# A two-layer diffusion block on one core: loads ahead of the first block in one row, filter network first, small loads and spectrum reloads on GpSimd's queue

## The chip, the core and the metric

The kernel runs on one core of a Trainium2 chip. The metric is device time in microseconds of one launch, the median of several runs. Before the change it is 1902.57 us (three runs, 1902.44 to 1904.87). One execution was also recorded by the hardware profiler; all rows of profiles are from such executions, and their times count from the first instruction of the span.

A core has five engines that run side by side, each with its own queue of instructions that it works off in order: TensorE (matmuls; PE in the profile, its weight loads PEld), VectorE (DVE), ScalarE (ACT), GpSimd (POOL) and SyncE (SP, which here only issues DMAs). ScalarE and GpSimd can issue DMAs too, each from its own queue. Engines wait for each other and for DMAs by semaphores.

## The reference, cut to what matters

Two token streams, `x` (256 tokens, "latent") and `ctx` (256 tokens), width 1024, go through two layers. Each layer is a half feed-forward block, a mixer and a second half feed-forward block. All in float32.

```python
s_l, s_c = silu(c), silu(c_ctx)
for layer in range(2):
    need_ctx = layer < 1
    mod_l = (s_l @ mod_w[layer] + mod_b[layer]).reshape(1, 9, 1, 1024)     # and mod_c from s_c
    lat = lat + 0.5 * mod_l[:, 2] * swiglu(adaln_in(lat, g[0], mod_l, 0), w1, w3, w2)   # same for ctx
    h_l = adaln_in(lat, g[1], mod_l, 1)                                    # same for ctx
    y_l, y_c = mixer_ab(h_l, h_c, ...) if layer == 0 else mixer_c(h_l, h_c, ...)
    lat = macaron(lat + mod_l[:, 5] * y_l, g[2], mod_l, 2, ...)            # ctx in layer 0 only
return rmsnorm(lat, final_norm_w)

def adaln_in(h, gain, mod, k):
    return rmsnorm(h, gain) * (1.0 + mod[:, 3 * k + 1]) + mod[:, 3 * k]

def hyena_filters(n, f_w0, f_b0, f_w1, f_b1, f_freq, f_wout):
    hid = sin(f_freq * (z @ f_w0 + f_b0))
    for i in range(2):
        hid = sin(f_freq * (hid @ f_w1[i] + f_b1[i]))
    return (hid @ f_wout).reshape(n, 2, 2, 512) * window

def long_conv_bidir(v, h_fwd, h_bwd, skip):          # used twice in mixer_ab, per stream
    taps_f = rfft(concat([h_fwd, 0, reversed h_bwd]), n=2 * n)
    return irfft(rfft(v, n=2 * n) * taps_f)[:n] + v * skip
```

The filters of the long convolution depend on weights alone, not on tokens, and so does the modulation (on `c`, `c_ctx` and the weights). Both can be computed before the first feed-forward block.

## The kernel before, in words

Activations stand transposed: width over the 128 partitions, in 8 chunks of 128, tokens along the row (512: latent, then context). The residual is the eight tiles `res`. For precision each float32 matmul of the big products is made of three in a faster format: every operand is split into a high and a low part (`split`, L149: ScalarE copies the high part at L151, VectorE subtracts at L152), and `mm3` (L154 to L157) multiplies high by high, high by low and low by high. That is why L155, L156 and L157 carry most of TensorE's time. Small or early products stay float32.

**The opening** is what comes ahead of `ffn(0, 0, ...)`, written at L1070 to L1092:

- constants and the filter network's inputs (`cst` L161, `w0` L171 to L173) are loaded by SyncE; rows of biases and of `c`, `c_ctx` into `crow` (L177, L179) by ScalarE; norm weights and biases into `prow` and `mrow` (L200, L214) mostly by GpSimd. Small transposes on TensorE (L182, L205, L216) turn them into columns; `fcol` (L184) holds the network's biases, `sF` (L187) the silu of `c`, `c_ctx`.
- `load_x(s)` (L329) loads 1 MB of one stream and transposes it into `res` (L335, L336). `Adaln.stats` (L464) computes the norm's scale: squares (L437), sums (L439), two matmuls, a power on GpSimd (L447).
- `mod_group` (L242) computes one eighth of the modulation rows 1 and 0: two loads of 512 KB (`mw`, L256) and per load two float32 matmuls that use 32 columns of TensorE each (L259), the profile counts four; the four column groups of the two loads differ. After eight groups the sums are gathered (`part` L264, L268) and `modT` is written (L233).
- `filter_hidden` (L359) is the filter network: three layers of matmul (L365, L367), range reduction on VectorE (L369 to L375) and sine on ScalarE (L378, L382). `filter_tables` (L345) loads the output weights `wo`, the window `win`, the skips and the transform tables. `filter_taps` (L389) makes the taps (L395 to L402), `filter_spectra` (L404) their spectra by matmuls, 60 in all, scales them (L418, L419, L425) and stores them to DRAM from ScalarE's queue (`TR`, `TI`, `TN`, L426 to L428).
- `ffn_first` (L521) loads and splits the first weights of the feed-forward block; `Adaln.stream(s)` (L467) writes its normalized input `h` (L482 to L484), which needs `modT`.

**After it** come the feed-forward blocks, 11 slices of 256 hidden columns each, with weights streamed by SyncE; the rest of the modulation is spread over them (`mod_row`, L271). In `mixer_ab` the spectra come back from DRAM: `tn` at L903 and L904, `tf` in `load_filters` at L787 and L788, both by SyncE, into the pool `fp` of three buffers; the products with the token spectra use them at L819 and L820.

**What sets the order.** The program names no order across engines and no addresses. A planner runs the whole program once on its own cost model with the numbers of buffers that the pools name (`bufs=`); then each engine's queue is ordered: of what is ready in the plan, first what the plan can least afford to delay. Loads are queued as soon as the plan has room for their tile, so `tn` is loaded back some 500 us before its use. Tiles get addresses from their planned lifetimes; two tiles whose planned lifetimes don't overlap may share memory, and then the later one's writer waits for the earlier one's readers.

Of the kernel before, what the change touches and what calls it, by code (L numbers as in the profile page):

```python
# [97 lines left out]
def tile_dit(ctx: ExitStack, tc: tile.TileContext, a: dict, out: bass.AP, dbg=None):  # L98
# [4 lines left out]
    big = ctx.enter_context(tc.tile_pool(name="big", bufs=1))  # L103
    wp = ctx.enter_context(tc.tile_pool(name="wp", bufs=4))
    hp = ctx.enter_context(tc.tile_pool(name="hp", bufs=8))
    gp = ctx.enter_context(tc.tile_pool(name="gp", bufs=10))
    mp = ctx.enter_context(tc.tile_pool(name="mp", bufs=6))
    fp = ctx.enter_context(tc.tile_pool(name="fp", bufs=3))
    tp = ctx.enter_context(tc.tile_pool(name="tp", bufs=NT))
    xp = ctx.enter_context(tc.tile_pool(name="xp", bufs=6))  # L110
    sp = ctx.enter_context(tc.tile_pool(name="sp", bufs=2))
# [81 lines left out]
    for nm, src, n in (  # L193
# [6 lines left out]
        (nc.scalar if nm == "nw" else nc.gpsimd).dma_start(prow[r : r + n, : src.shape[1]], src)  # L200
# [960 lines left out]
```

## Time and profile before

| what | value |
|---|---|
| median of three runs | 1902.57 us (1902.44 to 1904.87) |
| the profiled execution's own time | 1902.08 us |
| its span, first to last instruction | 1900.3 us |
| instructions | 25792 |
| busy share of TensorE, VectorE, ScalarE, GpSimd | 97%, 66%, 39%, 4% |
| bytes moved | 271.65 MB, mean 143 GB/s |
| granted clock of TensorE | 0.990 |

"Busy" is the share of the span in which an engine has an instruction in work; issuing DMAs does not count. Matmuls are pipelined and their ends are modelled, so that neighbours overlap in the rows. In rows of groups "x64 | 15.0, 604 | 2.9 <-DMA" reads: 64 instructions, together busy 15.0 us, mean of one 604 ns, and 2.9 us in which the engine stood idle just before them, ended by a DMA. In rows of waits "14.5, 7, 3.9" are total, number of times and longest wait in us. A DMA row ends with the size of each transfer and the median us from issue to landing.

### The profile page before, as it was taken

What the parts mean: (1) busy time and instruction counts of PE and PEld (TensorE: products, weight loads), DVE (VectorE), ACT (ScalarE), POOL (GpSimd) and SP (SyncE); (2) the same over time, 40 slices, a digit from 0 to 9 for tenths busy, and PEclk for the clock granted to TensorE, in tenths of its full rate; (3) what the DMA queues carried; (4) which work ended last, traced back from release to release, by engine and by line L of the source; (5) the groups of instructions that cost most, each with busy time, mean ns of one, the idle gap of its engine ahead of it and who ended that gap; (6) DMA issues with size and microseconds to landing.
All of it is one profiled execution on the core that took longest, in us unless ns stands there. A gap on an engine that the chain in (4) does not pass through costs nothing.

```text
span 1900.3 us, 25792 instructions
## 1 busy us (share of the span) xinstructions
PE 1850.6 (97%) x10358; PEld 1566.0 (82%) x10358; DVE 1257.0 (66%) x1972; ACT 738.0 (39%) x1190; POOL 73.6 (4%) x63
## 2 busy tenths in 40 slices
PE   7999999999999998999999999999999999989998
PEld 3868788889878788888888897887888988889998
DVE  5557686776666795877767358655344866667665
ACT  4533233224555433432332234222322566654443
POOL 1000000000100002000000110000000100020000
PEclk9999999999999999999999999999999999989998
DMA  8675555351323332545554325443323233335551
GB/s 267 216 245 177 171 186 208 127 191 45 122 88 100 104 109 84 195 170 175 197 184 143 111 78 176 173 160 113 111 89 119 54 106 84 106 111 178 200 188 57
DMA packets 191009, 271.65 MB, mean 143 GB/s; under 512 B 19688, under 2 KB 139755, under 8 KB 190889
## 3 DMA queue, kind: packets, MB, share of 16 engines
q1 hardware_dynamic: 189324, 267.63, 42.7%
q10 hardware_dynamic: 1260, 2.14, 0.3%
q8 instruction: 81, 1.33, 0.3%
q14 instruction: 40, 0.32, 0.1%
q0 software_dynamic: 304, 0.24, 0.0%
HBM read 262.63 MB, written 7.34 MB: 142 GB/s over the span
## 4 chain that ended last, share of the span: by engine, by line
PE 67%; DVE 4%; ACT 2%; issue 1%; POOL 1%; DMA 0%; SPq 0%; DVEq 0%; ACTq 0%
PE pu L155 11%; PE pu L156 11%; PE pu L157 11%; PE pd L155 7%; PE pd L157 7%; PE pd L156 7%; PE ps L155 3%; PE ps L156 3%; PE ps L157 3%; PE pu L1012 1%; DVE wl L152 1%; PE ps L667 1%; DVE acc L439 1%; PE pu L982 1%; PE ps L293 1%
## 5 line engine op out<-in xcount | busy, mean ns | idle before, releaser
L157 PE MATMUL pu<-h,wl 128*128 128x512 f32 (+1 forms) x1600 | 545.6, 342 | 3.0 <-POOL wl L152 3.0
L155 PE MATMUL pu<-h,wh 128*128 128x512 f32 (+1 forms) x1600 | 545.0, 342 | 1.6 <-ACT h L483 1.5
L156 PE MATMUL pu<-h,wh 128*128 128x512 f32 (+1 forms) x1600 | 546.0, 342 | 0.1
L151 ACT ACTIVATE wh<-raw 128x1024 fp32r<-128x1024 f32 x228 | 240.3, 1058 | 558.6 <-PE pu L156 403.2
L152 DVE TENSOR_TENSOR wl<-raw,wh 128x1024 fp32r<-128x1024 f32 x216 | 263.7, 1225 | 203.8 <-ACT wh L151 177.6
L155 PEld LDWEIGHTS pu<-h,wh 128*128 128x128 f32 x1600 | 303.8, 191 | 44.1 <-issue 4.2
L157 PEld LDWEIGHTS pu<-h,wl 128*128 128x128 f32 x1600 | 304.7, 191 | 38.4 <-POOL wl L152 3.3
L156 PEld LDWEIGHTS pu<-h,wh 128*128 128x128 f32 x1600 | 304.9, 191 | 33.8 <-DVE h L484 0.5
L282 DVE SCALAR_TENSOR_TENSOR mv<-mw,sF,mv 128x1024 f32<-128x1024 f32 x210 | 258.5, 1279 | 20.5 <-DMA mw<-in_mod_w_dram 16.2
L151 ACT ACTIVATE w<-raw 128x1024 fp32r<-128x1024 f32 x88 | 91.5, 1057 | 164.2 <-PE ps L156 120.5
L510 DVE SCALAR_TENSOR_TENSOR res<-pd,gate,res 128x256 f32<-128x256 f32 x244 | 110.7, 479 | 40.5 <-PE pd L157 40.0
L547 DVE TENSOR_TENSOR sg<-sg,pu 128x512 f32<-128x512 f32 (+1 forms) x87 | 52.2, 603 | 127.4 <-PE pu L157 125.0
L152 DVE TENSOR_TENSOR w<-raw,w 128x1024 fp32r<-128x1024 f32 x88 | 107.0, 1221 | 42.0 <-ACT w L151 41.9
L155 PE MATMUL pd<-g,w 128*128 128x512 f32 (+1 forms) x376 | 133.6, 355 | 0.0
L157 PE MATMUL pd<-g,w 128*128 128x512 f32 (+1 forms) x376 | 132.6, 353 | 0.0
L156 PE MATMUL pd<-g,w 128*128 128x512 f32 (+1 forms) x376 | 132.6, 353 | 0.0
L155 PE MATMUL ps<-g,w 128*128 128x512 f32 (+1 forms) x320 | 116.3, 363 | 0.0
L157 PE MATMUL ps<-g,w 128*128 128x512 f32 (+1 forms) x320 | 116.1, 363 | 0.0
L156 PE MATMUL ps<-g,w 128*128 128x512 f32 (+1 forms) x320 | 116.1, 363 | 0.0
L155 PE MATMUL pd<-h,wh 128*128 128x512 f32 (+1 forms) x288 | 108.3, 376 | 1.9 <-ACT e L989 0.9
L157 PE MATMUL pd<-h,wl 128*128 128x512 f32 (+1 forms) x288 | 107.6, 374 | 1.7 <-DVE wl L152 1.7
L156 PE MATMUL pd<-h,wh 128*128 128x512 f32 (+1 forms) x288 | 106.9, 371 | 0.0
(256 smaller groups left out, 2726.0 us busy)
## 6 DMA issues: line engine op xcount, KB each, us to landing
raw<-in_ffn_w_dram SPq DMA_DIRECT2D x132, 1024.0 KB, 5.3
mw<-in_mod_w_dram SPq DMA_DIRECT2D x144, 512.0 KB, 6.0
raw<-in_ab_w_in_dram SPq DMA_DIRECT2D x12, 1024.0 KB, 6.9
raw<-in_na_w_in_dram SPq DMA_DIRECT2D x12, 1024.0 KB, 5.0
raw<-in_ab_w_out_dram SPq DMA_DIRECT2D x4, 1024.0 KB
raw<-in_na_w_out_dram SPq DMA_DIRECT2D x4, 1024.0 KB, 5.5
bias<-in_na_rpb_dram SPq DMA_DIRECT2D x32, 96.0 KB, 6.1
dftr<-const_dft_dram SPq DMA_DIRECT2D x5, 256.0 KB
```

The lines of the kernel that those rows point to most:

```text
L151: S.activation(hi, src, AF.Copy)
L152: eng.tensor_tensor(lo, src, hi.bitcast(F32), op=ALU.subtract)
L155: nc.tensor.matmul(ps, wh, xh, start=start, stop=False)
L156: nc.tensor.matmul(ps, wh, xl, start=False, stop=False)
L157: nc.tensor.matmul(ps, wl, xh, start=False, stop=stop)
L282: V.scalar_tensor_tensor(acc, mw, c, acc, op0=ALU.mult, op1=ALU.add)
L293: nc.tensor.matmul(ps[32 * j : 32 * j + 32], row[:, 31 - b : 63 - b], mod_acc[l, i][j % 2][:, j // 2], start=b == 0, stop=b == len(batch) ...
L439: V.tensor_tensor(acc, acc, q, op=ALU.add)
L510: V.scalar_tensor_tensor(res[d][:, sl], ps[:, po], g[:, d, s : s + 1], res[d][:, sl], op0=ALU.mult, op1=ALU.add)
L547: V.tensor_tensor(sg[:, sl], sg[:, sl], p3[:, sl], op=ALU.mult)
L667: nc.tensor.transpose(at[kt // 2][:, o : o + P], e[:, P * kt : P * kt + P], ident)
L982: nc.tensor.matmul(pss[m], x[pr, qsl], y[pr], start=n == 0, stop=n == 2)
```

## The change

In words:

- The 16 loads of the modulation weights for rows 1 and 0 get two tiles of their own (pool `mwp`, 32 KB per partition each) and are written out ahead: eight for row 1 after `x`, the other eight after `ctx`. `mod_group` then finds its weights there. The loads of `x` and `ctx` are parted from their transposes (`load_x`, `take_x`).
- The filter network comes first, ahead of the transposes of `x`; the output weights and the window are loaded at the start from ScalarE's queue, the former in two loads in place of four. The modulation groups are spread by two, two, one, one, two between taps and spectra.
- `crow` and all of `prow` are loaded from GpSimd's queue; the two rows of `f_b1` in one load.
- `tn` and `tf` are loaded back by GpSimd in place of SyncE.
- The small constant tiles and `res` become slices of one tile `kept`. All other SBUF pools go through a wrapper that asks for addresses aligned to the size (up to 2048 bytes).

```diff
+class _Pool:
+    def tile(self, shape, dt, **kw):
+        size = 4 * math.prod(shape[1:])
+        if size >= 1024:
+            kw["align_bytes"] = min(size & -size, 2048)
+        return self.pool.tile(shape, dt, **kw)
...
+    mwp = _Pool(ctx.enter_context(tc.tile_pool(name="mwp", bufs=2)))
...
+    kept = const.tile([P, KEPT_W], F32, name="kept")
+    def keep(w):
+        used[0] += w
+        return kept[:, used[0] - w : used[0]]
...
-        nc.scalar.dma_start(crow[8 * s : 8 * s + 8, :P], src)
-    for r, src in ((16, a["hy_f_b0"]), (17, a["hy_f_b1"][0, 0:1]), (18, a["hy_f_b1"][0, 1:2]), (19, a["hy_f_freq"])):
-        nc.scalar.dma_start(crow[r : r + 1, :64], src)
+        nc.gpsimd.dma_start(crow[8 * s : 8 * s + 8, :P], src)
+    for r, src in ((16, a["hy_f_b0"]), (17, a["hy_f_b1"][0]), (19, a["hy_f_freq"])):
+        nc.gpsimd.dma_start(crow[r : r + src.shape[0], :64], src)
...
-        (nc.scalar if nm == "nw" else nc.gpsimd).dma_start(prow[r : r + n, : src.shape[1]], src)
+        nc.gpsimd.dma_start(prow[r : r + n, : src.shape[1]], src)
...
-    res = [big.tile([P, TOK], F32, name=f"res{d}") for d in range(NDC)]
+    res = [keep(TOK) for d in range(NDC)]
...
+    mod_rest = {}
+    def mod_load(l, i, g, mws=None):
+        mws = mws or [gp.tile([P, 2, 512], F32, tag="g", name="mw") for _ in range(2)]
+        for c in range(2):
+            k0 = 4 * (g % 2) + 2 * c
+            nc.sync.dma_start(mws[c], mod_rows(l, i, k0, 2, (512 * (g // 2), 512 * (g // 2) + 512)).rearrange("(k p) f -> p k f", p=P))
+        return mws
+    mwa = [mwp.tile([P, 8, 2, 512], F32, tag="mw", name="mw") for _ in range(2)]
+    def mod_ahead(n, l, i):
+        for g in range(4):
+            mod_rest[i, g] = mod_load(l, i, g, [mwa[g // 2][:, 4 * n + 2 * (g % 2) + c] for c in range(2)])
...
-        for c in range(2):
+        mws = mod_rest.pop((i, g), None) or mod_load(l, i, g)
+        for c, mw in enumerate(mws):
             k0 = 4 * (g % 2) + 2 * c
-            mw = gp.tile([P, 2, 512], F32, tag="g", name="mw")
-            nc.sync.dma_start(mw, mod_rows(l, i, k0, 2, (512 * (g // 2), 512 * (g // 2) + 512)).rearrange("(k p) f -> p k f", p=P))
...
-        wo = M(F32, name="wo")
-        for o in range(2):
-            for i in range(2):
-                nc.sync.dma_start(wo[o][64 * i : 64 * i + 64], a["hy_f_wout"][0][:, 1024 * o + 512 * i : 1024 * o + 512 * i + 512])
+        wo = mp.tile([P, 2, TOK], F32, tag="m", name="wo")
+        src = a["hy_f_wout"][0].rearrange("j (o i c) -> j o i c", o=2, i=2)
+        for i in range(2):
+            nc.scalar.dma_start(wo[64 * i : 64 * i + 64], src[:, :, i])
         win = fp.tile([P, 2, TOK], F32, tag="f", name="win")
-        nc.sync.dma_start(win, a["win"].rearrange("p (a c) -> p a c", a=2))
+        nc.scalar.dma_start(win, a["win"].rearrange("p (a c) -> p a c", a=2))
...
-                nc.sync.dma_start(tf[o, f][0], TR[o][f])
-                nc.sync.dma_start(tf[o, f][1], TI[o][f])
+                nc.gpsimd.dma_start(tf[o, f][0], TR[o][f])
+                nc.gpsimd.dma_start(tf[o, f][1], TI[o][f])
...
-            nc.sync.dma_start(tn[o][1:], TR[o][0][1:])
-            nc.sync.dma_start(tn[o][0:1], TN[o])
+            nc.gpsimd.dma_start(tn[o][1:], TR[o][0][1:])
+            nc.gpsimd.dma_start(tn[o][0:1], TN[o])
...
-    load_x(0)
-    mod_some(1)
-    load_x(1)
-    ads[0, 0].stats(0)
-    mod_some(1)
-    ads[0, 0].stats(1)
-    hid = filter_hidden(w0)
-    mod_some(1)
-    mod_some(1)
-    mod_some(1)
-    flt = filter_tables()
-    filter_taps(0, PU, hid, *flt)
-    mod_some(1)
-    filter_taps(1, PU, hid, *flt)
-    mod_some(1)
-    mod_some(1)
-    filter_spectra(0, (0,), PU, flt[-1])
-    first = ffn_first(0, 0)
-    ads[0, 0].stream(0)
-    filter_spectra(0, (1,), PU, flt[-1])
-    filter_spectra(1, (0,), PU, flt[-1])
-    filter_spectra(1, (1,), PU, flt[-1])
-    ads[0, 0].stream(1)
+    xin = load_x(0)
+    flt = filter_tables()
+    mod_ahead(0, 0, 1)
+    cin = load_x(1)
+    mod_ahead(1, 0, 0)
+    hid = filter_hidden(w0)
+    take_x(0, xin)
+    mod_some(2)
+    take_x(1, cin)
+    ads[0, 0].stats(0)
+    ads[0, 0].stats(1)
+    filter_taps(0, PU, hid, *flt)
+    mod_some(2)
+    filter_taps(1, PU, hid, *flt)
+    filter_spectra(0, (0,), PU, flt[-1])
+    mod_some(1)
+    filter_spectra(0, (1,), PU, flt[-1])
+    mod_some(1)
+    first = ffn_first(0, 0)
+    filter_spectra(1, (0,), PU, flt[-1])
+    mod_some(2)
+    ads[0, 0].stream(0)
+    filter_spectra(1, (1,), PU, flt[-1])
+    ads[0, 0].stream(1)
```

More of the change, by code (lines that the diff above doesn't have):

```diff
@@ L44 @@
 CST_W = _n
+KEPT_W = CST_W + NDC * TOK + 920
 def constants():
@@ L102, in tile_dit @@
     const = ctx.enter_context(tc.tile_pool(name="const", bufs=1))
[L103 to L111, printed above, removed]
+    wp = _Pool(ctx.enter_context(tc.tile_pool(name="wp", bufs=4)))
+    hp = _Pool(ctx.enter_context(tc.tile_pool(name="hp", bufs=8)))
+    gp = _Pool(ctx.enter_context(tc.tile_pool(name="gp", bufs=10)))
+    mp = _Pool(ctx.enter_context(tc.tile_pool(name="mp", bufs=6)))
+    fp = _Pool(ctx.enter_context(tc.tile_pool(name="fp", bufs=3)))
+    tp = _Pool(ctx.enter_context(tc.tile_pool(name="tp", bufs=NT)))
+    mwp = _Pool(ctx.enter_context(tc.tile_pool(name="mwp", bufs=2)))
+    xp = _Pool(ctx.enter_context(tc.tile_pool(name="xp", bufs=6)))
+    sp = _Pool(ctx.enter_context(tc.tile_pool(name="sp", bufs=2)))
     pu = ctx.enter_context(tc.tile_pool(name="pu", bufs=4, space=PSUM))
@@ L157, in mm3 @@
         nc.tensor.matmul(ps, wl, xh, start=False, stop=stop)
-    cst = const.tile([P, CST_W], F32, name="cst")
+    kept = const.tile([P, KEPT_W], F32, name="kept")
+    used = [0]
+    def keep(w):
+        used[0] += w
+        return kept[:, used[0] - w : used[0]]
+    cst = keep(CST_W)
     nc.sync.dma_start(cst, a["cst"])
@@ L165, in tile_dit @@
     wf = cst[:, _CO["wf"]]
-    ones = const.tile([P, 1], F32, name="ones")
+    ones = keep(1)
     V.memset(ones, 1.0)
-    nhalf = const.tile([P, 32], F32, name="nhalf")
+    nhalf = keep(32)
     V.memset(nhalf, -0.5)
@@ L176, in tile_dit @@
     for s, src in enumerate((a["c"].rearrange("o (k p) -> (o k) p", p=P), a["c_ctx"].rearrange("(k p) -> k p", p=P))):
-        nc.scalar.dma_start(crow[8 * s : 8 * s + 8, :P], src)
-    for r, src in ((16, a["hy_f_b0"]), (17, a["hy_f_b1"][0, 0:1]), (18, a["hy_f_b1"][0, 1:2]), (19, a["hy_f_freq"])):
-        nc.scalar.dma_start(crow[r : r + 1, :64], src)
+        nc.gpsimd.dma_start(crow[8 * s : 8 * s + 8, :P], src)
+    for r, src in ((16, a["hy_f_b0"]), (17, a["hy_f_b1"][0]), (19, a["hy_f_freq"])):
+        nc.gpsimd.dma_start(crow[r : r + src.shape[0], :64], src)
     pst = PS()
     nc.tensor.transpose(pst[:, :20], crow[:20, :P], ident[:20, :20])
-    fcol = const.tile([P, 4], F32, name="fcol")
+    fcol = keep(4)
     V.tensor_copy(fcol, pst[:, 16:20])
-    sF = const.tile([P, NDC, 38], F32, name="sF")
+    sF = keep(NDC * 38).rearrange("p (k f) -> p k f", k=NDC)
     V.memset(sF, 0.0)
@@ L217, in tile_dit @@
         V.tensor_copy(modb[:, l], pst[:, :72])
-    res = [big.tile([P, TOK], F32, name=f"res{d}") for d in range(NDC)]
-    modT = [const.tile([P, 72, 2], F32, name=f"modT{l}") for l in range(2)]
+    res = [keep(TOK) for d in range(NDC)]
+    modT = [keep(144).rearrange("p (k s) -> p k s", s=2) for l in range(2)]
     def raw():
@@ L331, in load_x, with take_x @@
         nc.sync.dma_start(xin, a[("x", "ctx")[s]][0].rearrange("(t p) c -> p t c", p=P))
+        return xin
+    def take_x(s, xin):
         for d in range(NDC):
@@ L356, in filter_tables @@
         tables(2, lambda i: tab[i][0], lambda i: tab[i][1])
-        return wo, [win[:, 0], win[:, 1]], skip, tab
+        return [wo[:, 0], wo[:, 1]], [win[:, 0], win[:, 1]], skip, tab
     def filter_hidden(w0):
@@ L519, in span, with ffn_first @@
         return slice(LAT * streams[0], LAT * streams[-1] + LAT)
-    def ffn_first(l, j, eng=V):
-        r1, r3 = [wload(a[nm][l, j][:, :FB]) for nm in ("ffn_w1", "ffn_w3")]
+    def ffn_first(l, j, eng=V, rs=None):
+        r1, r3 = rs or [wload(a[nm][l, j][:, :FB]) for nm in ("ffn_w1", "ffn_w3")]
         return [whalf(r[:, :, P * c : P * c + P], "w", eng=eng) for c in range(2) for r in (r1, r3)]
```

14 lines of the change are left out of this document (7 added, 7 removed).

## The prediction

> **What bounds the kernel now.** I read the page first (busy time, slices, chain), then the first 130 us by stages, then the groups of TensorE and the queue waits of the opening, and last the places where moved loads are used. Times are microseconds of the profiled execution.
>
> ```profile
> span 1900.3 us, 25792 instructions
> PE 1850.6 (97%) x10358; PEld 1566.0 (82%) x10358; DVE 1257.0 (66%) x1972; ACT 738.0 (39%) x1190; POOL 73.6 (4%) x63
> PE   7999999999999998999999999999999999989998
> PE 67%; DVE 4%; ACT 2%; issue 1%; POOL 1%; DMA 0%; SPq 0%; DVEq 0%; ACTq 0%
> ```
>
> TensorE is busy 97% of the span and carries the chain that ended last; DMA has 0% of that chain. Only the first slice is below 8. So a change in the loads can pay in the opening and hardly anywhere else. The same table of busy time, cut by hand at the first matmul, the first filter tap and the first matmul of the first feed-forward block (columns: stretch, length, then busy us and count of PE, PEld, DVE, ACT, POOL; granted clock, DMA share, GB/s):
>
> ```profile
> 0.00:7.68 7.68, 0.00 (x0) 0.00 (x0) 0.71 (x5) 0.47 (x1) 3.53 (x10) 1.00 0.58 175
> 7.68:33.38 25.70, 20.38 (x107) 10.56 (x107) 13.49 (x42) 14.30 (x42) 2.40 (x4) 1.00 0.87 297
> 33.38:63.58 30.20, 30.20 (x108) 15.98 (x109) 20.22 (x36) 15.83 (x26) 0.00 (x0) 0.94 0.76 243
> 63.58:1900.30 1836.72, 1800.06 (x10146) 1539.46 (x10144) 1222.59 (x1890) 707.34 (x1123) 67.71 (x49) 0.99 0.42 139
> ```
>
> The first block starts at 63.58. Before it TensorE waits 7.68 for its first operand, then is idle 25.70 − 20.38 = 5.32, and from the first tap on it is never idle: 30.20 of 30.20. The opening is therefore bound by TensorE from 33.38 on, and before that by what it waits for. The granted clock is 0.94 in the last stage; at full clock the same work would take about 30.20 × 0.06 = 1.8 less. What the work is, in the groups of TensorE up to 63.58 and, last row, of the stage from 33.38 on:
>
> ```profile
> L259 PE MATMUL ps<-mw,sF 128*32 128x512 f32 x64 | 15.0, 604 | 2.9 <-DMA mw<-in_mod_w_dram 2.9
> L395 PE MATMUL pu<-wo,hid 128*128 128x512 f32 x16 | 9.3, 727 | 0.2 <-PE ps L259 0.2
> L335 PE MATMUL pu<-cst,raw 128*128 128x128 f32 x32 | 6.1, 348 | 0.8 <-ACT sq L437 0.8
> L365 PE MATMUL pd<-w 33*64 33x256 f32 x2 | 1.1, 657 | 7.7 <-DMA w<-const_tmp_dram 7.7
> L268 PE MATMUL ps<-cst,part 128*128 128x8 f32 x8 | 1.0, 255 | 0.0
> L259 PE MATMUL ps<-mw,sF 128*32 128x512 f32 x24 | 6.3, 604 | 0.0
> ```
>
> Modulation (L259) costs 15.0 and the taps (L395) 9.3, clock loss included. The 60 spectrum matmuls take what is left of the last stage: 30.2 − 9.3 − 6.3 − 1.0 = 13.6, or 0.227 each. The longest idle time inside the opening, 2.9 of the 5.32, is for modulation weights. Why they come late stands in the waits of SyncE's own queue in the first 50 us:
>
> ```profile
> SPq L256 <- PE ps L259: 14.5, 7, 3.9
> SPq L256 <- DMA mw<-in_mod_w_dram: 8.5, 4, 3.7
> SPq L256 <- DMA crow<-in_c_ctx_dram: 2.2, 1, 2.2
> SPq L161 <- DMA crow<-in_c_dram: 2.0, 1, 2.0
> ```
>
> SyncE stands still 14.5 because the place a modulation load is to fill is still being read by a matmul, 8.5 behind earlier loads, and 4.2 behind two loads of 4 KB that ScalarE issued.
>
> **The change part by part.**
>
> *Loads in a row.* In the changed kernel the 16 modulation loads of this stage (512 KB each) have two tiles of 32 KB per partition to themselves, so the 14.5 goes. What must land before the last modulation matmul, from the DMA issues up to 130 us:
>
> ```profile
> mw<-in_mod_w_dram SPq DMA_DIRECT2D x28, 512.0 KB, 6.0
> raw<-in_x_dram SPq DMA_DIRECT2D x1, 1024.0 KB, 5.5
> raw<-in_ctx_dram SPq DMA_DIRECT2D x1, 1024.0 KB
> wo<-in_hy_f_wout_dram SPq DMA_DIRECT2D x4, 128.0 KB
> win<-const_win_dram SPq DMA_DIRECT2D x1, 512.0 KB, 7.1
> dftr<-const_dft_dram SPq DMA_DIRECT2D x2, 256.0 KB
> cst<-const_cst_dram SPq DMA_DIRECT2D x1, 133.0 KB
> ```
>
> 16 × 512 + 2 × 1024 + 512 + 512 + 512 + 133 KB and some 70 KB of small ones are 12.3 MB. At the 297 GB/s of the second stage that takes 41 us, at that rate divided by its 0.87 share 36. From about 2 us on, the last one lands between 38 and 43. Today:
>
> ```profile
> 13.22 1.07 PE L259 MATMUL ps<-mw,sF 128*32 128x512 f32 x8
> 51.49 1.05 PE L259 MATMUL ps<-mw,sF 128*32 128x512 f32 x4
> 57.31 1.69 ACT L483 ACTIVATE h<-xr,modT 128x256 fp32r<-128x256 f32 x4
> 63.58 0.19 PEld L155 LDWEIGHTS pu<-h,wh 128*128 128x128 f32 x1
> ```
>
> The last modulation matmuls start at 51.49, and 57.31 − 51.49 = 5.8 later the first normalized activation is written. With the loads at 38 to 43 that would be at 44 to 49, well before TensorE is through with its other work. So DMA is not the next bound; the work of TensorE is: 20.38 + 30.20 = 50.6, or 48.8 at full clock.
>
> *Idle time of TensorE.* Of the 5.32, the 2.9 for modulation weights goes. The rest is small waits in the network and the statistics. New ones come: the filter network now runs first, and its three layers hang on each other. Today:
>
> ```profile
> 10.08 0.53 DVE L369 TENSOR_SCALAR fx<-pd,fcol 64x256 f32<-64x256 f32 x1
> 12.81 0.28 DVE L375 TENSOR_SCALAR fx<-fx 64x256 f32<-64x256 f32 x1
> 29.20 0.06 DVE L384 MEMSET hid<- 64x1 f32 x1 [0.81 <-ACT hid L383]
> ```
>
> One layer needs 13.1 − 10.1 = 3.0 on VectorE to which I allow 1.4 for sine, matmul and hand-overs; three layers of 4.4 and some 2 for the last copies, from 10.1, end near 25 rather than at 29.26. Until then TensorE has transposes (6.1) and about half of the modulation (7.5) to fill 7.68 to 25, some 14 to 16 with the small matmuls: 1 to 3 idle. I take 2.0, so 3.3 of idle time goes; the ends are 0 (new waits as long as the old) and 5.3.
>
> *Clock.* The 1.8 lost today follows on the idle time in front of the taps. A thinly used stage in front of them remains, only shorter. I take half, 0.9; the ends are a loss of 1.8 more and a gain of 1.8.
>
> *Modulation matmuls side by side.* The eight of one group (two loads) took 1.07 when both loads were there (13.22); four of one load take 1.05 (51.49). So two loads done together cost what one costs alone. In the last stage 24 took 6.3, six lots of 1.05: all apart. With both loads of a group at home, 8 × 1.07 = 8.6 in place of 15.0 would be possible, a gain of 6.4. The planner, however, puts single lots between other matmuls as it expects each load. I take a third, 2.2; the ends are 0 and 6.4.
>
> *Small loads to GpSimd.* SyncE's 4.2 go; that is contained in the loads' times above. In exchange the network's biases wait for GpSimd, whose rows of the first 6 us and of the two skip loads are:
>
> ```profile
> 1.29 1.30 POOL L214 DMA_DIRECT2D mrow<-in_mod_b_dram  x2 [0.84 <-POOLq L1144]
> 2.58 0.50 POOL L200 DMA_DIRECT2D prow<-in_final_norm_w_dram  x1
> skip<-in_hy_bias_dram POOLq DMA_DIRECT2D x2, 2.0 KB, 6.2
> ```
>
> If the two of mrow still go first, five loads of 0.50 end at 5.1 and the last lands about 6 later, near 11, against a first use at 10.08: the network may be 1 late, which the idle time above has room for; 0 lost, ends 0 and 1. Queued behind them on GpSimd are prow and mrow, used by the adaptive norms only, some 40 us later. The filter weights, the window and the biases on ScalarE and GpSimd ask for 1.0 MB earlier than today, inside the 12.3 MB. Nothing is added to compute; merged constants are the same bytes.
>
> *Reloads of spectra.* Twelve issues go from SyncE to GpSimd: eight of tf, four of tn. In the opening SyncE no longer stands behind them; TensorE did not wait for the weights queued there (no idle time from 33.38 to 63.58), so 0. The late ones matter more:
>
> ```profile
> 664.52 0.42 SPq L788 DMA_DIRECT2D tf<-TI  x1
> 671.43 0.69 DVE L819 TENSOR_TENSOR u<-pu,tf 128x512 f32<-128x512 f32 x1 [0.26 <-PE pu L157]
> tf<-TI SPq DMA_DIRECT2D x2, 256.0 KB, 7.4
> ```
>
> The last is issued at 664.52 and the second stage's products start at 671.43 with the half that was asked for earlier; landing took 7.4 on SyncE's queue in the opening, 6.2 for a small load on GpSimd's. I take 0, ends −1 and +2. On GpSimd only the norm powers and the halves of weights could queue behind them.
>
> [...]
>
> *Sum.* 3.3 + 0.9 + 2.2 = 6.4, so the first block starts near 57.2. Everything after it is shifted: with TensorE busy 1800.06 of 1836.72 there, no slack swallows it. Its own 1836.72 − 1800.06 = 36.7 of idle time can change as the planner orders anew; I put that at 0 ± 3. Against the profiled execution's 1902.08 (span 1900.3 and 1.8 around it) that is 1895.7; the median of the runs shown is 1902.57, 0.5 above that execution, so **1896.2**.
>
> **The rivals.**
>
> *All lots pair up.* Idle time falls to 1.0, the clock stays full and all eight groups run as one lot each: 4.3 + 1.8 + 6.4 = 12.5, time 1890.1. For it: the lot of eight at 13.22. Against it: the six single lots in a stage in which TensorE always had other work.
>
> *The last modulation groups become the tail.* In the text of the changed kernel the last two groups stand behind three quarters of the spectra. If TensorE takes them there, the 5.8 to the first activation has only the last 12 spectrum matmuls as cover, 12 × 0.227 = 2.7: 3.1 are given back, 1899.3. Against it: the loads are there some 10 us earlier, and the planner puts first what it can least afford to delay.
>
> *Slower: TensorE stands in its own queue behind loads.* It issues in the planned order. If that holds the 16 lots early and the loads are slower than planned, taps and spectra stand behind them though their data is there. At 272 GB/s, the rate of the first 50 us,
>
> ```profile
> 0.00:50.00 50.00, 37.00 (x152) 16.71 (x154) 25.17 (x65) 20.50 (x52) 5.93 (x14) 0.97 0.83 272
> ```
>
> 12.3 MB end at 45 + 2 = 47, plus 1 for the last lot; with all taps and spectra behind (9.3 + 13.6) the block starts at 71, 7.4 later than now: 1910. It decides from the point where more than 63.6 − 48 = 15.6 of that work stands behind the last lot. For it: 2.9 of such waiting today. Against it: the network runs first, so taps are ready by 25.
>
> *The loads are not freed.* The two tiles of 32 KB need room that other tiles hold, and SyncE would wait for it as now: 1902.6. Against it: the activations and weight halves that fill most room are written only when modulation is done.
>
> **How the numbers follow.** Chances: forecast 0.55, all pair up 0.18, tail 0.10, slower 0.10, not freed 0.07. The forecast's own range is 1893 to 1899. About 0.2%, 3.8 us, is what a measurement of this kernel can tell from no change. Faster by more: 0.52 of the forecast's 0.55, the 0.18, and a third of the tail, together 0.74. Within: 0.16. Slower: 0.10. The range goes to 1888, below which only the best of the first rival lies, and up to 1905, above which most of the slower case lies.
>
> **What will show it.** In the changed profile: SyncE's waits on L259 gone in the opening; the last L259 lot before 46; the network's end (L384) near 25; L259's busy time between 8.6 and 15; TensorE's idle time from 7.7 to the first block near 2; the first matmul on h near 57. I am wrong if that row is at 57 and the time has not moved (then stalls later took it back), if L259's last lot is late though its loads landed, or if the tf products near 671 wait on DMA.

## The result, and the profile after

The changed kernel takes **1914.62 us** (median of four runs, 1910.77 to 1917.60); the kernel before, run beside it, 1902.51 (1902.18 to 1904.87). The ratio is 1.0060 with a 95% interval of 1.0038 to 1.0082: slower by 12.1, where 6.4 less was forecast. The profiled execution took 1916.38, its span 1914.6. Of the executions of all programs below, two were slow (10311.95 us in e6, 9635.34 in e11) and stand in no ratio.

In the changed kernel's line numbers L293 is the modulation matmul (L259 before), L267 its load, L298 and L302 gather its sums, L402 and L404 are the network's matmuls, L406 to L421 the rest of the network, L432 the taps, L455 to L465 the scaling and storing of spectra, L372 the transposes of `x` and `ctx`, L519 to L521 write `h`, L161 and L162 are `split`, L165 to L167 `mm3`.

The page's head of the changed kernel:

```profile
span 1914.6 us, 25737 instructions
PE 1853.8 (97%) x10358; PEld 1569.5 (82%) x10358; DVE 1259.1 (66%) x1972; ACT 734.6 (38%) x1190; POOL 81.9 (4%) x81
```

The table of busy time, cut at the first matmul, the first tap and the first matmul on `h`, as before (columns: stretch, length, busy us and count of PE, PEld, DVE, ACT, POOL; granted clock, DMA share, GB/s):

```profile
0.00:9.83 9.83, 0.00 (x1) 0.04 (x1) 0.70 (x5) 1.28 (x1) 5.87 (x15) 1.00 0.82 253
9.83:38.25 28.42, 20.54 (x86) 10.00 (x87) 12.11 (x37) 11.44 (x33) 2.37 (x5) 0.89 0.75 274
38.25:70.96 32.71, 28.83 (x129) 17.19 (x129) 19.69 (x36) 19.25 (x35) 4.39 (x7) 0.97 0.72 242
70.96:1914.60 1843.64, 1804.41 (x10144) 1542.22 (x10144) 1226.60 (x1895) 702.60 (x1122) 69.26 (x55) 0.99 0.41 137
```

The first block starts at 70.96, not 63.58 (+7.4), and what follows takes 1843.64, not 1836.72 (+6.9). TensorE's idle time before the block is 9.83 + 7.88 + 3.88 = 21.6 where it was 13.0: the wait for the first operand is 2.2 longer, the stretch up to the taps has 2.6 more, and the stretch from the taps on, never idle before, has 3.9. TensorE's waits for loads in the first 72 us (the waits of the tail stand in the rows further down):

```profile
PE pd L402 <- DMA w<-const_tmp_dram: 9.8, 1, 9.8
PE pu L372 <- DMA raw<-in_ctx_dram: 3.3, 1, 3.3
PE ps L223 <- DMA prow<-in_diff_subln_w_dram: 1.8, 1, 1.8
```

No wait for modulation weights is left, and that part came true. Of the 3.9, 1.8 + 1.5 are the tail: two waits between the last spectra and the first block. TensorE from 60 us on, spectrum matmuls left out, and ScalarE in the same time:

```profile
61.68 1.92 PE L293 MATMUL ps<-mw,kept 128*32 128x512 f32 x14
...
68.37 1.06 PE L302 MATMUL ps<-kept,part 128*128 128x8 f32 x8 [1.83 <-ACT part L298]
70.96 0.58 PE L165 MATMUL pu<-h,wh 128*128 128x256 f32 x1 [1.53 <-ACT h L520]
```

```profile
61.31 2.00 ACT L161 ACTIVATE wh<-raw 128x1024 fp32r<-128x1024 f32 x2
65.08 0.69 ACT L455 ACTIVATE tr<-pu,kept 128x512 f32<-128x512 f32 x1 [1.77 <-DMA TR<-tr]
65.67 1.05 ACT L161 ACTIVATE wh<-raw 128x1024 fp32r<-128x1024 f32 x1
...
67.75 0.57 ACT L298 ACTIVATE part<-ps 128x512 f32<-128x512 f32 x1
...
70.40 2.10 ACT L520 ACTIVATE h<-xr,kept 128x256 fp32r<-128x256 f32 x5 [0.94 <-DVE xr L519]
```

The last modulation matmuls end at 61.68 + 1.92 = 63.6; only twelve spectrum matmuls come behind them. The copy of the sums, `part`, then stands in ScalarE's queue behind weight halves and spectra until 67.75, and the first `h` comes at 70.40. For most of the 1.77 ahead of the spectrum at 65.08 ScalarE stood idle with the sums complete: that spectrum waited for a store to land, and `part` stood behind it. The loads had landed by about 44, some 18 us before those matmuls; two stretches, DMA share in the last but one column:

```profile
42.00:44.00 2.00, 2.00 (x9) 0.62 (x11) 2.00 (x6) 0.73 (x2) 0.00 (x0) 1.00 0.84 325
44.00:46.00 2.00, 2.00 (x14) 0.69 (x7) 1.81 (x4) 0.79 (x2) 0.00 (x0) 1.00 0.03 10
```

The network ends later, at 33.6 instead of 29.26. On VectorE its second step (L408) comes behind the copy of the row tile (L224), which waited for the small loads on GpSimd's queue:

```profile
14.88 0.29 DVE L224 COPY kept<-ps 128x128 f32<-128x128 f32 x1 [2.95 <-PE ps L223]
15.09 0.28 DVE L408 TENSOR_SCALAR fn<-fx 64x256 f32<-64x256 f32 x1
...
33.55 0.06 DVE L421 MEMSET hid<- 64x1 f32 x1 [0.81 <-ACT hid L420]
```

The third part of the loss is the clock. TensorE's full first 1890 us, of the kernel before and of the changed one:

```profile
0.00:1890.00 1890.00, 1845.60 (x10336) 1561.55 (x10336) 1255.14 (x1969) 733.82 (x1182) 72.94 (x62) 0.99 0.43 143
```

```profile
0.00:1890.00 1890.00, 1835.96 (x10216) 1552.58 (x10217) 1247.54 (x1947) 725.05 (x1169) 81.19 (x80) 0.99 0.42 143
```

Idle time is 1890 − busy: 44.4 before, 54.0 after, 9.6 more, of which 8.6 lie ahead of the first block. For the clock I summed busy time × (1 − clock) over windows of 10 us: 10.8 before, 17.9 after, 7.1 more: 4.1 before 90 us, 1.6 from there to 620, 3.5 between 620 and 800, and 2.1 less after that. Against these 16.7 stand 3.3 less work of TensorE ahead of the block, 2.8 of it in the modulation matmuls, which now run side by side (below): 13.4, where the span grew by 14.3.

### The profile page after: what moved, and what is told of

Same layout as the page of the kernel before. It is cut to its first block, busy times and chain, and to the rows that moved or that the text cites. A ratio compares the mean times of both kernels' runs of the same rounds, so it can differ in the third digit from the quotient of the medians.

```text
span 1914.6 us, 25737 instructions
## 1 busy us (share of the span) xinstructions
PE 1853.8 (97%) x10358; PEld 1569.5 (82%) x10358; DVE 1259.1 (66%) x1972; ACT 734.6 (38%) x1190; POOL 81.9 (4%) x81
## 4 chain that ended last, share of the span: by engine, by line
PE 49%; issue 11%; DVE 2%; ACT 1%; POOL 1%; DVEq 0%; POOLq 0%; ACTq 0%
PE pu L165 8%; PE pu L167 8%; PE pu L166 8%; PE pd L165 5%; PE pd L166 5%; PE pd L167 5%; PE ps L165 2%; PE ps L166 2%; PE ps L167 2%; PE pu L1049 1%; PE ps L327 1%; PE pu L1019 1%; DVE acc L476 1%; POOL wl L162 0%; ACT wh L161 0%
## 5 line engine op out<-in xcount | busy, mean ns | idle before, releaser
L167 PE MATMUL pu<-h,wl 128*128 128x512 f32 (+1 forms) x1600 | 546.9, 343 | 3.0 <-POOL wl L162 3.0
L165 PE MATMUL pu<-h,wh 128*128 128x512 f32 (+1 forms) x1600 | 545.9, 343 | 3.3 <-ACT h L520 3.1
L161 ACT ACTIVATE wh<-raw 128x1024 fp32r<-128x1024 f32 x228 | 240.9, 1060 | 618.0 <-PE pu L166 524.5
L162 DVE TENSOR_TENSOR wl<-raw,wh 128x1024 fp32r<-128x1024 f32 x216 | 264.6, 1227 | 228.5 <-ACT wh L161 207.7
L165 PEld LDWEIGHTS pu<-h,wh 128*128 128x128 f32 x1600 | 304.9, 192 | 46.0 <-issue 4.2
L167 PEld LDWEIGHTS pu<-h,wl 128*128 128x128 f32 x1600 | 306.0, 191 | 38.5 <-POOL wl L162 3.2
L316 DVE SCALAR_TENSOR_TENSOR mv<-mw,kept,mv 128x1024 f32<-128x1024 f32 x210 | 258.4, 1277 | 14.5 <-DMA mw<-in_mod_w_dram 14.5
L161 ACT ACTIVATE w<-raw 128x1024 fp32r<-128x1024 f32 x88 | 91.3, 1053 | 140.7 <-PE ps L166 133.6
L547 DVE SCALAR_TENSOR_TENSOR kept<-pd,gate,kept 128x256 f32<-128x256 f32 x244 | 110.4, 478 | 45.1 <-PE pd L167 44.1
L165 PE MATMUL pd<-g,w 128*128 128x512 f32 (+1 forms) x376 | 133.2, 354 | 0.0
L167 PE MATMUL pd<-g,w 128*128 128x512 f32 (+1 forms) x376 | 132.3, 352 | 0.0
L162 DVE TENSOR_TENSOR w<-raw,w 128x1024 fp32r<-128x1024 f32 x88 | 106.8, 1219 | 23.2 <-ACT w L161 22.9
L165 PE MATMUL ps<-g,w 128*128 128x512 f32 (+1 forms) x320 | 116.2, 363 | 0.0
L167 PE MATMUL ps<-g,w 128*128 128x512 f32 (+1 forms) x320 | 116.0, 363 | 0.0
L165 PE MATMUL pd<-h,wh 128*128 128x512 f32 (+1 forms) x288 | 108.4, 376 | 1.7 <-ACT u L980 0.9
L167 PE MATMUL pd<-h,wl 128*128 128x512 f32 (+1 forms) x288 | 107.6, 373 | 2.4 <-DVE wl L162 2.4
```

Source lines behind the costliest of these rows:

```text
L161: S.activation(hi, src, AF.Copy)
L162: eng.tensor_tensor(lo, src, hi.bitcast(F32), op=ALU.subtract)
L165: nc.tensor.matmul(ps, wh, xh, start=start, stop=False)
L167: nc.tensor.matmul(ps, wl, xh, start=False, stop=stop)
L316: V.scalar_tensor_tensor(acc, mw, c, acc, op0=ALU.mult, op1=ALU.add)
L547: V.scalar_tensor_tensor(res[d][:, sl], ps[:, po], g[:, d, s : s + 1], res[d][:, sl], op0=ALU.mult, op1=ALU.add)
```

## The experiments

One table for all runs. "Homes" are the two tiles of their own that the modulation weights have in the changed kernel. "Against before" is the difference of the medians, each to the kernel before in the same series, then the ratio with its interval. "Network" is when the last hidden values are written, "block" the first matmul on `h` (63.8 for the kernel before, whose weight load is the row at 63.58). Idle, lost clock and full-speed work are TensorE's up to that matmul: idle is the time less the busy time; lost clock is busy × (1 − clock), summed over windows of 1 us; work is the rest. Differences of the medians under 4 us are near what the measurement can tell.

| kernel | against before, us | ratio | network | block | idle | lost clock | work |
|---|---|---|---|---|---|---|---|
| before | | | 29.3 | 63.8 | 13.0 | 1.6 | 49.2 |
| after | +12.1 | 1.0060 [1.0038, 1.0082] | 33.6 | 71.0 | 21.6 | 3.5 | 45.9 |
| e1 modulation ahead of spectra | +0.4 | 1.0000 [0.9991, 1.0010] | 33.9 | 65.5 | 18.3 | 1.6 | 45.6 |
| e2 homes not shared | +13.7 | 1.0059 [1.0040, 1.0078] | 33.6 | 72.4 | 23.2 | 4.8 | 44.4 |
| e3 both | +0.5 | 1.0003 [0.9993, 1.0012] | 33.6 | 66.5 | 19.2 | 3.9 | 43.4 |
| e4 reloads on SyncE | +13.2 | 1.0064 [1.0047, 1.0082] | 33.5 | 73.1 | 24.0 | 2.6 | 46.5 |
| e5 e1, `ctx` early | +4.1 | 1.0026 [1.0016, 1.0036] | 39.6 | 69.1 | 15.0 | 4.6 | 49.5 |
| e6 e1, `wo`, `win` on SyncE | −0.3 | 0.9999 [0.9990, 1.0008] | 34.3 | 66.0 | 16.2 | 3.2 | 46.5 |
| e7 e5, small loads on ScalarE | +10.5 | 1.0057 [1.0043, 1.0070] | 35.6 | 67.1 | 13.8 | 3.4 | 49.9 |
| e8 e7 and e6 | +4.6 | 1.0029 [1.0019, 1.0040] | 43.4 | 69.0 | 17.6 | 4.6 | 46.8 |
| e9 homes, old order | +10.0 | 1.0058 [1.0044, 1.0072] | 27.9 | 65.7 | 16.8 | 2.5 | 46.4 |
| e10 network first | +2.7 | 1.0013 [1.0004, 1.0022] | 27.1 | 68.5 | 15.7 | 4.5 | 48.4 |
| e11 its operand first | +3.5 | 1.0022 [1.0012, 1.0032] | 32.8 | 65.7 | 16.5 | 3.4 | 45.9 |
| e12 one tile, `ctx` earlier | +3.9 | 1.0023 [1.0014, 1.0033] | 40.0 | 69.2 | 14.7 | 4.8 | 49.6 |
| e13 tail filled | +11.1 | 1.0054 [1.0041, 1.0068] | 33.5 | 70.7 | 18.9 | 1.7 | 50.2 |
| e14 network first, `wo` on SyncE | +2.4 | 1.0012 [1.0001, 1.0023] | 29.8 | 65.8 | 17.8 | 2.8 | 45.3 |
| e15 e1, small loads on ScalarE | +1.3 | 1.0003 [0.9995, 1.0012] | 35.9 | 66.7 | 16.7 | 4.6 | 45.4 |

**e1: all modulation ahead of the spectra.**

```diff
     filter_taps(1, PU, hid, *flt)
+    mod_some(4)
     filter_spectra(0, (0,), PU, flt[-1])
-    mod_some(1)
...
-    mod_some(1)
...
-    mod_some(2)
```

> The changed kernel with its last four modulation groups written ahead of the spectra; nothing else moves in the opening (TensorE's order is the same up to the eleventh lot of L293, which now all stand before the first spectrum). Theory A, the tail: the last seven lots ran at 61.68, behind 48 of 60 spectrum matmuls, and the 4.0 us of idle time from 66.4 to 70.96 and the half clock behind it (about 2.7) are its price; then the first block starts near 66.5 and the time falls by 5 to 7, to about 1908 to 1910. Theory B, loads that wait for shared memory: the lots are late for their loads and nothing is gained, 1913 to 1916. Theory C, the loss is the spectrum reloads on GpSimd: the same, 1913 to 1916.

Busy time of e1 in the cuts from above, and TensorE's row of its last modulation lots:

```profile
0.00:9.75 9.75, 0.00 (x0) 0.03 (x1) 0.70 (x5) 1.28 (x1) 5.53 (x15) 1.00 0.84 254
9.75:37.04 27.29, 19.22 (x87) 9.62 (x87) 12.10 (x37) 11.44 (x33) 2.71 (x5) 0.94 0.71 263
37.04:65.50 28.46, 27.95 (x131) 17.34 (x130) 21.83 (x42) 18.32 (x35) 1.66 (x2) 1.00 0.70 246
65.50:1899.30 1833.80, 1798.16 (x10145) 1536.61 (x10143) 1223.22 (x1889) 702.94 (x1123) 72.60 (x60) 0.99 0.41 139
```

```profile
49.47 1.46 PE L293 MATMUL ps<-mw,kept 128*32 128x512 f32 x10
```

With four groups moved up, the last lots end at 50.9 instead of 63.6, spectra cover the way to `h`, and the time falls by some 11 (10.5 between the medians, 11.7 against the kernel before in each series) to that of the kernel before; 5 to 7 were expected. So with the order of the last four groups undone, the whole loss against before is gone, and e2 and e3 below show the same once more (+13.7 and +0.5). It is not the whole miss: the forecast gain of 6.4 isn't there either. In e1 the idle time is 5.3 above before, and the work 3.6 below.

**e2, e3: homes that share no memory.** In the changed kernel SyncE's sixth modulation load waits for readers of small tiles of the start, with which a home shares its memory (the first two rows; the third is `ctx`'s load):

```profile
SPq L267 <- DVE acc L476: 4.4, 1, 4.4
SPq L267 <- DMA mrow<-in_mod_b_dram: 4.2, 1, 4.2
SPq L365 <- PE pd L404: 6.3, 1, 6.3
```

e2 writes a column of both homes at the very start, so that they get memory of their own; e3 does so on top of e1.

```diff
+    for w in mwa:
+        V.memset(w[:, :, :, 0:1], 0.0)
```

> The changed kernel with one column of each of the two modulation tiles set to zero at the start, so that the plan has them live from there and no opening tile can lie in the same memory. SyncE's sixth modulation load then no longer waits for eight small loads and a VectorE sum (4.2 + 4.4 us in the changed kernel); the load of the context still waits for a filter matmul. Theory B: the first loads end 6 to 9 earlier, the idle 7.9 of TensorE from 9.83 to 38.25 shrinks by 3 to 6 and the time by as much, 1909 to 1912. Theory A: the tail stays where it is, what is won is idle again behind the last lots, 1913 to 1916. Theory C: 1913 to 1916.

> Both edits of the two runs above: modulation groups ahead of the spectra, and the two modulation tiles live from the start. Theory A alone: as with the first edit, 1908 to 1910. Theories A and B, adding: first block near 62, 1903 to 1906. Theory C: 1913 to 1916.

SyncE's first loads of the homes and of `ctx`, in the changed kernel and in e2:

```profile
10.71 11.83 SPq L267 DMA_DIRECT2D mw<-in_mod_w_dram  x6
28.89 0.37 SPq L365 DMA_DIRECT2D raw<-in_ctx_dram  x1
```

```profile
10.36 3.53 SPq L267 DMA_DIRECT2D mw<-in_mod_w_dram  x6
28.90 0.37 SPq L367 DMA_DIRECT2D raw<-in_ctx_dram  x1
```

The six loads are issued in 3.5 instead of 11.8, and nothing is won: the next load on the queue, `ctx`, is issued at 28.9 in both, because its tile waits for a matmul of the network (L404 in the changed kernel: 6.3 there, 14.5 in e2). e3 adds nothing to e1.

**e4: the reloads of spectra back on SyncE.** `tf` and `tn` as in the kernel before, all else as changed.

> The changed kernel with tn and tf loaded back by SyncE as before; TensorE's order in the opening stays the same. Theory C: the time falls by 5 or more, to 1905 to 1910, with the first block where it is near 71. Theories A and B: no change beyond 2 us, 1912 to 1917; the first block near 71.

The time is the same (1.0064 of the kernel before, 1.0060 with the reloads on GpSimd's queue). No engine waits for `tf` to land, in the kernel before with SyncE's queue or in the changed one with GpSimd's: VectorE's products with `tf` wait 1.1 there and 0.8 here, all of it for matmuls. Which queue lands sooner the traces don't show: of the eight loads of `tf` in e4 the four from `TI` have no landing on record, and those from `TR` a median of 15.2. From GpSimd's queue, in the changed kernel, they landed in 2.9 to 6.5.

**e5 to e8: one late load after the other.** All contain e1.

```diff
     xin = load_x(0)
+    cin = load_x(1)                      # e5, e7, e8
     flt = filter_tables()
     mod_ahead(0, 0, 1)
-    cin = load_x(1)
...
-        nc.gpsimd.dma_start(crow[...], src)          # e7, e8; so for norm_w in prow
+        nc.scalar.dma_start(crow[...], src)
...
-            nc.scalar.dma_start(wo[...], src[:, :, i])      # e6, e8; so for win
+            nc.sync.dma_start(wo[...], src[:, :, i])
```

> On top of e1 (all modulation ahead of the spectra), the load of ctx is issued right behind that of x, ahead of the sixteen modulation loads in homes. Theory C: without the tail, what is left of the missing gain is the load of ctx: in e1 it is issued only at 28.9 us, TensorE stands idle 3.1 us for it at 34.1, and its transposes then stand ahead of the first taps at 37.0. Then idle time of TensorE between the first network operand and the first taps falls from 8.1 to about 5, the first FFN block begins near 62.5 (65.5 in e1), and the time is 1901 (1904.1 in e1, 1903.7 before). Rival D, the network sets the first taps: its hidden values are ready only at 33.8, so TensorE idles elsewhere instead; first taps stay within 1 us of 37.0, the block at 65, time 1903.5 to 1905.

> On top of e1, the loads of the filter's last layer and of its window go back from ScalarE's queue to SyncE's. Theory N: on ScalarE's queue they are issued at once and share the 16 DMA engines with the first operand of the network, which then lands at 9.8 instead of 7.7 us, and the whole opening is late by these 2.1. Then the first matmul comes near 8, the first FFN block near 63.5 and the time is 1902 (2 under e1). Rival: the first operand is late because more loads are issued ahead of it at all (the GpSimd ones too); first matmul stays at 9.5 to 10, time 1904 to 1906, and worse where the last layer's load is now late for the taps.

> e5 and, besides, the rows of c, ctx's c, the biases and norm weights go back to ScalarE's queue, as before the change. Theory S: on the GpSimd queue these small loads land late (the row tile at 14.7 us, TensorE waits 2.1 for it, VectorE 3.3, and the network's second layer stands behind that copy on VectorE). Then the copy comes 4 us earlier, the network ends near 30.5 (33.8 in e1), the first taps come near 33.5, and the time is 1.5 to 3 below e5: 1898 to 1900 if theory C holds too. Rival: the queue of the small loads makes no difference (within 1 us of e5), because the network waits on TensorE's order and not on these.

> e7 and the two filter loads of e6 on SyncE's queue as well, so that of the change remain: one tile for what is kept, homes for sixteen loads, GpSimd reloads of the spectra. If theories C, N and S add, the first operand lands near 8, the first block comes near 59 to 60 and the time is 1896 to 1898, below the kernel before (1903.7) and close to what was forecast of the change. If the network or the modulation matmuls set the block anyhow, the time is that of the best of e5 to e7.

Of e5 the network's end; of e6 TensorE's wait for the first operand:

```profile
39.52 0.06 DVE L421 MEMSET hid<- 64x1 f32 x1 [0.81 <-ACT hid L420]
```

```profile
PE pd L402 <- DMA w<-const_tmp_dram: 7.0, 1, 7.0
```

Each wait went that was meant to go, and the time didn't follow. In e5 the wait for `ctx` is gone, but with `ctx` at hand the planner puts its transposes and statistics ahead of the network's second and third layer, which ends at 39.6. In e6 the first operand comes 2.8 earlier and the block is where it was. Theories C (`ctx`'s load), N (the first operand beside `wo` and `win`) and S (the small loads) all name real waits and none of them the bound. Adding them (e8) is no better than e5. e7 shows the stall move behind the block: its first matmul is at 67.1, and 3.1 us of waiting for `h` from ScalarE follow it.

**e9 to e12: homes in the old order, the network first, one tile.** e9 has the calls and the queues of the kernel before, with the homes and their loads written ahead, the one tile `kept` and the merged loads of `wo`; e10 and e11 are e1 with `filter_hidden(w0)` written ahead of `load_x(0)`, e10 with the small loads on ScalarE and `wo`, `win` on SyncE, e11 with `filter_tables()` behind `take_x(0, xin)`; e12 has neither homes nor new queues, only the one tile `kept`, the alignment and the merged loads of `wo`; but its edit also writes the load of `ctx` ahead of the transposes of `x` and of the first modulation group.

> The order and the queues of the kernel before; of the change remain the two home tiles for sixteen modulation loads, the one tile for what is kept, and the merged loads of the filter's last layer. It tests the sum of the forecast by itself: SyncE's waits for modulation buffers gone, lots pairing up, nothing else moved. Theory (homes are worth what was forecast): 1897 to 1898. Theory P (the end of the filter network sets the last spectrum): in all runs so far the last spectrum ends the later the later the network's last hidden values are written (29.3 and 63.8 before, 33.8 and 65.5 in e1, 39.5 and 69.1 in e5); the homes only help as far as the network isn't delayed by them, so the last spectrum ends at 62 to 65 and the time is 1901 to 1905.

> e1, and the filter network written ahead of the load of x; its small loads on ScalarE's queue and the filter's last layer and window on SyncE's queue, as before. Theory P: the network then ends at 29 to 31 (33.8 in e1), the last spectrum at 61 to 63 and the time is 1898 to 1901. Rival (TensorE's order or the loads set the last spectrum): it stays within 1 us of 65.5, time 1903 to 1905.

> e1, and the filter network written ahead of the load of x, whose first operand so stands ahead of x on SyncE's queue, and the filter's tables taken after the transposes of x; the small loads stay on the GpSimd queue. Theory P: the first matmul comes near 7.5 to 8, the network ends near 31, the last spectrum near 63, time 1900 to 1902. Rival (the row tile on the GpSimd queue holds the network as in e1, from 14.7 on): network ends near 33, time 1903 to 1905.

> Neither homes nor new queues nor the new order: of the change only the one tile for what is kept, the alignment of tiles and the merged loads of the filter's last layer remain. Control: if these cost nothing, the time is that of the kernel before, 1902.5 to 1905, the network ends at 29 to 30 and the first FFN block comes near 63.6. Rival: the plan that the new placing of the tiles leads to is itself later; time 1906 or more, and all runs of the change carry that price.

Of e9 the stretch from 90 to 200 us and TensorE's one wait for loads in it; of e10 and e12 the end of the network:

```profile
90.00:200.00 110.00, 104.41 (x445) 76.41 (x446) 68.67 (x79) 34.30 (x41) 0.00 (x0) 0.97 0.57 193
```

```profile
PE ps L293 <- DMA mw<-in_mod_w_dram: 5.3, 1, 5.3
```

```profile
27.05 0.06 DVE L421 MEMSET hid<- 64x1 f32 x1 [0.81 <-ACT hid L420]
```

```profile
39.97 0.06 DVE L420 MEMSET hid<- 64x1 f32 x1 [0.81 <-ACT hid L419]
```

Theory P (the end of the network sets the block) falls with e10: the network ends at 27.1, earlier than in the kernel before, and the block still starts at 68.5. With the homes in the old order (e9) the block comes at 65.7, later than before, and at 100 us TensorE waits another 5.3 for a later modulation load; both times expected of e9 are missed by 8 or more. e12, meant as the control, is 3.9 slower (interval above 1). SyncE's rows for `ctx` and the modulation loads around it, in the kernel before and in e12:

```profile
7.26 0.89 SPq L256 DMA_DIRECT2D mw<-in_mod_w_dram  x2
8.20 0.47 SPq L331 DMA_DIRECT2D raw<-in_ctx_dram  x1
```

```profile
6.76 0.43 SPq L364 DMA_DIRECT2D raw<-in_ctx_dram  x1
7.24 1.66 SPq L267 DMA_DIRECT2D mw<-in_mod_w_dram  x3
```

In e12 `ctx` goes ahead of the modulation loads, its squares are summed ahead of the network's second layer (20.8 against 29.1 on VectorE), and the network ends at 40.0. In e5, which also writes `ctx` earlier, it ends at 39.6 and the block is at 69.1. So e12 doesn't separate the new placing of the tiles from the earlier load; what the tiles alone cost isn't shown.

**e13 to e15: what was still open.** e13 is the changed kernel with eighteen useless matmuls in its tail; e14 is e10 with the small loads on GpSimd; e15 is e1 with them on ScalarE.

```diff
     filter_spectra(1, (1,), PU, flt[-1])
+    fill = PD()
+    (fa, fb), (ga, gb) = flt[-1][0], taps[1][0][0]
+    for i in range(6):
+        mm3(fill, fa[:, :P], fb[:, :P], ga, gb, i == 0, i == 5)
     ads[0, 0].stream(1)
```

> The changed kernel with its tail, and eighteen matmuls of 128x512 whose result nobody reads, that stand on TensorE between the last spectrum and the last modulation matmul, where it sat idle (66.5 to 71.0 us). Theory K: TensorE's clock is halved from 70 to 76 us because it sat idle just before; with the stretch filled the clock stays at 1.0 there and the time falls by 2 to 2.5 us, to 1912, though 4 us of useless work were added. Rival: the clock is cut for another reason (or by the plan of the program), stays at 0.5 from 70 to 76, and the time is the same or up to 4 us longer: 1914.6 to 1918.

> e10, but the small loads stay on the GpSimd queue: e1 with the filter network written ahead of the load of x and the filter's last layer and window on SyncE's queue. If what is left of the forecast is kept away by the late first operand, the first matmul comes near 7.2, idle time and lost clock before the first FFN block come to 17 or less together (19.9 in e1) and the time is 1900 to 1902. Rival: the gain at the start is given back later in the opening, as in e6 and e10; time 1903.5 to 1906.

> e1 with the small rows alone back on ScalarE's queue. If the late row tile (TensorE 2.1 us, VectorE 3.3) holds the opening, its transpose comes before 11 us, the network ends near 30.5 (33.8) and the time is 1901 to 1902. Rival: the network is held by other work next (the statistics of x on VectorE), time within 1.5 us of e1's 1904, either side.

Three stretches of 3.41 us from the last spectra on, in the changed kernel, and the last two of them in e13:

```profile
65.95:69.36 3.41, 1.58 (x11) 1.13 (x9) 1.23 (x1) 3.41 (x6) 1.14 (x3) 1.00 0.69 199
69.36:72.77 3.41, 1.66 (x6) 1.30 (x6) 3.30 (x12) 2.20 (x6) 0.55 (x1) 0.50 0.67 160
72.77:76.18 3.41, 3.41 (x17) 3.41 (x17) 3.41 (x9) 1.71 (x4) 0.00 (x0) 0.50 1.01 319
```

```profile
69.36:72.77 3.41, 1.75 (x11) 1.17 (x10) 3.41 (x12) 2.11 (x5) 0.00 (x0) 0.99 1.07 398
72.77:76.18 3.41, 3.41 (x18) 3.41 (x18) 3.41 (x10) 1.31 (x3) 0.52 (x1) 0.51 1.05 408
```

With the idle stretch filled, the clock stays full from 69.36 to 72.77 (0.99), where it was halved (0.50). The second half-clock stretch remains (0.51); two short waits, 0.95 and 0.70, are left ahead of it at 69.8 to 72.1. So the first of them did come from the idle tail. The time is 1.1 lower, where 2 to 2.5 were expected, and these runs can't tell 1.1 from none. e14 starts TensorE at 6.9; e15 has the row tile on VectorE at 13.1 instead of 14.9, but its first operand only at 11.1; neither is below the kernel before.

No version beats both kernels: e1, e3, e6 and e15 can't be told from the kernel before, and all are faster than the changed one.

## Why the prediction was wrong, step by step

**The order of the last groups: the step that failed.** The prediction named this as a rival, "the last modulation groups become the tail", and gave it 0.10 against "the planner puts first what it can least afford to delay". The planner did take the last groups where they were written, with twelve spectrum matmuls as cover as the rival said. It is also a sign of being wrong that the prediction had named: the last lot late though its loads had landed. Its price was mis-sized too: 3.1 given back of a gain of 6.4 became, by e1 against the changed kernel, some 11. Two things were missing. ScalarE's queue lay between the last lot and `h`, so the way from the start of the last lot (63.6 − 1.05) to the first `h` at 70.40 was 7.9 instead of 5.8. Behind the idle tail the clock was halved (0.50) for another 6.8 us, of which TensorE was busy 5.1, so 2.5 lost. With the block 5.5 later than in e1 (70.96 against 65.50) that makes 8; the other 3 of the 11 these runs don't account for.

**Idle time of TensorE, −3.3: wrong, +5.3 without the tail (e1).** The 2.9 for modulation weights went as forecast. In its place came, all in e1's waits, 2.1 more for the first operand, 2.1 for the row tile and 3.1 for `ctx`; the other 0.9 is small waits. The prediction allowed the small loads "0 lost, ends 0 and 1", because it counted when the network needs `crow`; it took `prow` and `mrow` to be needed "some 40 us later", but their transposes and copies stand in the same queues ahead of the network. And it counted the MB of the window and output weights without asking whose turn they take: `tmp` lands 2.2 later beside them, which e6 shows. That the queue of the small loads decides is not shown: e15 gave no gain, and its first operand was later still.

**Network near 25: wrong,** 33.6; and where it did end early (e10, 27.1) it didn't help.

**Clock, −0.9: wrong sign,** +1.9 before the block, +4 by 90 us, +7.1 over the program. "Half" of 1.8 had no ground: a stretch of 3.4 us ran wholly at half clock or not at all (last section), so the loss in the stretch at 33.56, busy throughout, could only stay or go whole.

**Lots side by side, −2.2 of 6.4: the mechanism was right, the size somewhat small.** The modulation matmuls take 15.0 before and, at full clock, 12.2 after: 2.8 less (2.9 in e1). All work up to the block is 3.3 lower after, 3.6 in e1. But it isn't a gain of time. Block less lost clock is 62.2 before and 62.1 to 64.5 in all twelve runs without the tail, though their work differs by 6.5: what lots save, TensorE spends waiting. So "bound by TensorE from 33.38 on" described one trace and not a floor that less work would lower. What keeps the 62 isn't found: not the six modulation loads that e2 frees, the network's end (e10), the first operand (e6, e14) or `ctx` (e5) by itself. To hold the planned order fixed and change one load would tell; that wasn't tried.

**Everything after it shifted, 0 ± 3: wrong by +6.9.** About 2.5 of it is the half clock behind the tail. Another 3.5 is clock lost in addition between 620 and 800 us (6.2, before 2.7); it isn't shown to come from the change, for e13, with nearly the same order, loses 3.1 there. In e1 the same stretch is 2.9 shorter than before.

**Loads landed between 38 and 43: nearly right** (about 44). **Reloads 0: right,** by e4 (+13.2 against before, +12.1 with the reloads on GpSimd's queue); VectorE's products with `tf` wait 0.8 in the changed kernel, all of it for matmuls. **Slower, "TensorE stands in its own queue behind loads":** it gave 71 for the block, which is what was measured, but by luck: no modulation matmul waited for a load in the opening. **Not freed:** the shared homes did delay SyncE, and in e2, without that, nothing is won.

## What to carry to other kernels

A load that lands earlier pays only if its consumer is moved ahead too: look for what stands last in the program order between the loaded data and the next block, and price the whole queue of each engine on that way. Where a planner orders the engines, one call moved in the text moves more than itself: with `ctx`'s load written earlier the network ended at 39.6 in e5 and at 40.0 in e12. So a control with only the new tiles must leave every load in its old place, and it belongs ahead of any credit or blame for the loads; here that is missing. And idle time that one edit takes away must be followed to the next wait; here five named waits were removed one by one, and the opening became no shorter than before.
